# Feed-forward products by one level of Strassen's algorithm, in 1024-token blocks, with activations and weight sums kept in DRAM

## The chip, the cores and the metric

The kernel runs on one core of one Trainium2 chip. The metric is the device time of one execution in microseconds (us), here the median of three runs. The engines are TensorE (PE in the rows, PEld for its weight loads), VectorE (DVE), ScalarE (ACT), GpSimd (POOL) and SyncE (SP, which only issues DMAs). Each engine works through its own instructions in order.

## The reference, cut to what matters

One layer of a decoder trunk with 1024 features, on 2048 tokens with 16 learned tokens ahead of them. Three token mixers and an output projection come first, then the gated feed-forward part, which the change touches. All is float32.

```python
def hybrid_layer(x, ...):
    ...
    x = layer_norm(ALPHA * x + mix, ln1_g, ln1_b)
    u = causal_dwconv(x @ w_up, w_ffn_conv, b_ffn_conv)     # 3 taps, 2 x 2816 channels
    gate, val = jnp.split(u, 2, axis=-1)
    ffn = (jax.nn.silu(gate) * val) @ w_down                # 2816 -> 1024
    return layer_norm(ALPHA * x + ffn, ln2_g, ln2_b)
```

## The kernel before

**Products.** A float32 operand is split into two parts of a rounded type, hi and lo: ScalarE writes hi by a cast (L85), VectorE writes lo by a subtraction (L86); this is `split`. A product of two such operands is three matmuls (`mm3`, L90 to L92): hi by hi, hi by lo, lo by hi, added up in one PSUM bank of 512 columns. Weights come in units of 1024 values per partition (512 KB) by SyncE's queue, three units deep, and are split in halves of 512.

**Mixers.** Four blocks of 512 tokens run through the input projection, the recurrences and the output projection. The output projection and first layer norm of a block come while the next block is at work; that of the last block stands behind all others, in `run_last`. The normalised rows go to a DRAM array `x1`. GpSimd computes in this part alone.

**Feed-forward part.** Per block b of 512 tokens: `load_tokens` reads x1 back and transposes it on TensorE (`transpose_rows`, L172) into eight feature-major tiles `xhi`, `xlo`. `up` makes 22 pairs of a gate tile and a value tile of 128 channels, each 8 contraction tiles by 3 matmuls; in block 0 each is cut in two (258 and 256 columns), since two earlier tokens are needed for the convolution. The convolution's newest tap is ScalarE's (L659), the two others VectorE's (L655), both from the PSUM bank; then swish (L694), a product (L696), and a split into `ahi`, `alo` (for the last eight tiles `chi`, `clo`), all in SBUF. `down` multiplies these with w_down in two halves of 512 output columns, 22 contraction tiles by 4 row tiles by 3 matmuls each, adds to the rows of x1 (L714), and normalises (L194 to L202). In the last block the second half goes in two groups of two row tiles.

**Order.** TensorE's instructions stand in the order in which the program emits them. The other engines' instructions are placed by a scheduler by priority; weights are moved ahead (AHEAD), layer norms behind (BEHIND). `load_tokens(0)` is emitted ahead of `run_last`, so that TensorE works on the last output projection, then at once on `up(0)`.

Of the kernel before, what the change touches and what calls it, by code (L numbers as in the profile page):

```python
# [3 lines left out]

# [19 lines left out]
NB = 4  # L24
# [18 lines left out]


def bcast_rows(row, n):
    """A [1, C] DRAM row read by n partitions."""
    return bass.AP(row.tensor, row.offset, [[0, n], row.ap[-1]])


class Common:  # L50
    """What both phases use: float32r splitting, weight stream, transposes, products, layer norm.

    A float32 operand is split exactly into two float32r parts, hi + lo; a product is
    hi*hi + hi*lo + lo*hi, accumulated in float32.
    """

    def __init__(self, ctx, tc):
# [3 lines left out]
        self.act = ctx.enter_context(tc.tile_pool(name="act", bufs=1))  # L61
        self.wpool = ctx.enter_context(tc.tile_pool(name="w", bufs=3))
        self.rows = ctx.enter_context(tc.tile_pool(name="rows", bufs=5))
# [30 lines left out]
    def load_unit(self, src):  # L94
        """1024 weight values per partition; split in two halves, each in its own step."""
# [62 lines left out]
    def transpose_rows(self, src, t0, n, c0):  # L158
# [4 lines left out]
        nc = self.nc  # L163
        r = min(n, P)
        for k in range(KT):
            if k % 2 == 0:
                xs = self.row_tile().rearrange("p (t c) -> p t c", t=TT)
                nc.scalar.dma_start(
                    xs[0:r, 0:n // r, :], src[t0:t0 + n, k * P:(k + 2) * P].rearrange("(t p) c -> p t c", p=r))
            pt = self.bank()  # L170
            for t in range(n // r):
                nc.tensor.transpose(  # L172
                    pt[:, t * r:(t + 1) * r], xs[0:r, t, (k % 2) * P:(k % 2 + 1) * P], self.ident[0:r, 0:r])
            self.split(self.xT_hi[k][:, c0:c0 + n], self.xT_lo[k][:, c0:c0 + n], pt[:, 0:n])
# [646 lines left out]
```

## Time and profile before

| | us |
|---|---|
| median of three runs (2444.98 to 2448.37) | 2445.55 |
| the profiled execution, first to last instruction | 2445.3 |
| mixers, until the first transpose of `load_tokens(0)` | 885.3 |
| `load_tokens(0)` on TensorE | 15.0 |
| output projection of the last block | 45.4 |
| up, block 0 / each of blocks 1 to 3 | 249.9 / 244.6 |
| down, each of blocks 0 to 2 | 123.2 |
| last down with what follows it | 134.0 |

The page gives the busy time of each engine and the chain of work that ended last. The stages were found from TensorE's timeline, on which each changes its tiles' names, and a table by windows then gives each engine's busy time in each of them. Durations of single instructions come from groups by line and shape. A matmul's own duration includes its pipeline; its pace is the length of a stage over its count.

### The profile page before, as it was taken

To read this page: it belongs to the slowest core of one execution; us is meant where nothing else is said; L and a number is where in the kernel's file an instruction comes from. 1 tells how busy PE (TensorE), PEld (TensorE's weight loads), DVE (VectorE), ACT (ScalarE), POOL (GpSimd) and SP (SyncE) were. 2 spreads that over 40 slices of the span, in tenths; PEclk is the share of its full clock that TensorE was granted. 3 is DMA by queue.
4 is the path that set the end of the run, shared out by engine and by line. 5 is a ranking of instruction groups with operands and counts; after the bars stand their busy time and mean duration, and the time that the engine had idled before them with its cause. 6 is when DMAs were issued, how large, how long until landed. Compare 5 with 4: busy or idle time off the path is not lost.

```text
span 2445.3 us, 33339 instructions
## 1 busy us (share of the span) xinstructions
PE 2410.0 (99%) x12692; PEld 2018.5 (83%) x12692; DVE 1579.6 (65%) x2981; ACT 904.5 (37%) x1646; POOL 318.7 (13%) x351
## 2 busy tenths in 40 slices
PE   8999999999999989999999999999999999999998
PEld 6898777788888879999988888888888888888886
DVE  5676768678867957777635766634766634766636
ACT  3234323422432233554423444422444422444423
POOL 4351424143333310000000000000000000000000
PEclk9999999999999999999999999999999999999999
DMA  5112224322422343422322422322422322422234
GB/s 193 67 60 100 70 70 139 121 78 70 159 93 77 111 132 117 159 96 89 122 94 105 154 95 94 125 93 96 163 94 97 123 95 90 158 96 95 94 109 163
DMA packets 79439, 266.30 MB, mean 109 GB/s; under 512 B 8424, under 2 KB 16896, under 8 KB 79280
## 3 DMA queue, kind: packets, MB, share of 16 engines
q1 hardware_dynamic: 58032, 211.31, 25.0%
q10 hardware_dynamic: 20192, 50.54, 6.0%
q0 software_dynamic: 1056, 2.33, 0.5%
q8 instruction: 99, 1.62, 0.3%
q14 instruction: 60, 0.49, 0.1%
HBM read 247.31 MB, written 16.84 MB: 108 GB/s over the span
## 4 chain that ended last, share of the span: by engine, by line
PE 93%; DVE 3%; POOL 1%; issue 1%; DMA 1%; ACT 0%; DVEq 0%; ACTq 0%; POOLq 0%
PE bank L90 29%; PE bank L91 29%; PE bank L92 29%; PE bank L393 3%; DVE w_lo L86 1%; PE bank L406 1%; PE bank L476 1%; POOL pw L554 1%; PE bank L455 0%; PE bank L477 0%; DVE xlo L86 0%; DVE row L200 0%; DMA row<-x 0%; POOL work L418 0%; POOL work L419 0%
## 5 line engine op out<-in xcount | busy, mean ns | idle before, releaser
L86 DVE TENSOR_TENSOR w_lo<-w_raw,w_hi 128x512 fp32r<-128x512 f32 x806 | 588.2, 730 | 734.1 <-ACT w_hi L85 726.5
L85 ACT CAST w_hi<-w_raw 128x512 fp32r<-128x512 f32 x806 | 499.1, 619 | 1292.4 <-PE bank L92 652.4
L90 PE MATMUL bank<-xhi,w_hi 128*128 128x512 f32 (+3 forms) x2400 | 847.1, 353 | 0.0
L91 PE MATMUL bank<-xlo,w_hi 128*128 128x512 f32 (+3 forms) x2400 | 840.8, 350 | 0.0
L92 PE MATMUL bank<-xhi,w_lo 128*128 128x512 f32 (+3 forms) x2400 | 837.7, 349 | 0.1
L90 PEld LDWEIGHTS bank<-xhi,w_hi 128*128 128x128 f32 x2400 | 452.1, 188 | 64.4 <-issue 0.5
L92 PEld LDWEIGHTS bank<-xhi,w_lo 128*128 128x128 f32 x2400 | 452.0, 188 | 62.3 <-DVE w_lo L86 0.6
L91 PEld LDWEIGHTS bank<-xlo,w_hi 128*128 128x128 f32 x2400 | 451.6, 188 | 60.8 <-issue 0.7
L655 DVE SCALAR_TENSOR_TENSOR y<-bank,f_taps,y 128x256 f32<-128x256 f32 (+4 forms) x528 | 288.4, 567 | 16.3 <-ACT y L659 14.9
L90 PE MATMUL bank<-w_hi,chi 128*128 128x512 f32 (+1 forms) x528 | 211.7, 401 | 0.0
L92 PE MATMUL bank<-w_hi,clo 128*128 128x512 f32 (+1 forms) x528 | 208.0, 394 | 0.0
L91 PE MATMUL bank<-w_lo,chi 128*128 128x512 f32 (+1 forms) x528 | 207.5, 393 | 0.0
L90 PE MATMUL bank<-w_hi,ahi 128*128 128x512 f32 x448 | 177.8, 397 | 0.6 <-DVE xlo L86 0.2
L92 PE MATMUL bank<-w_hi,alo 128*128 128x512 f32 x448 | 177.0, 395 | 0.0
L91 PE MATMUL bank<-w_lo,ahi 128*128 128x512 f32 x448 | 177.0, 395 | 0.0
L659 ACT ACTIVATE y<-bank,f_bias,f_taps 128x512 f32<-128x512 f32 (+1 forms) x220 | 151.2, 690 | 23.9 <-PE bank L92 23.8
L90 PE MATMUL bank<-w_hi,xhi 128*128 128x512 f32 x272 | 112.0, 412 | 7.5 <-ACT xhi L85 7.5
L92 PEld LDWEIGHTS bank<-w_hi,clo 128*128 128x128 f32 (+1 forms) x528 | 97.9, 185 | 24.6
L91 PEld LDWEIGHTS bank<-w_lo,chi 128*128 128x128 f32 (+1 forms) x528 | 98.2, 186 | 22.8
L90 PEld LDWEIGHTS bank<-w_hi,chi 128*128 128x128 f32 (+1 forms) x528 | 98.2, 186 | 21.2
L92 PE MATMUL bank<-w_hi,xlo 128*128 128x512 f32 x272 | 107.7, 396 | 0.0
L91 PE MATMUL bank<-w_lo,xhi 128*128 128x512 f32 x272 | 107.5, 395 | 0.0
(165 smaller groups left out, 2279.5 us busy)
## 6 DMA issues: line engine op xcount, KB each, us to landing
w_raw<-in_w_up_dram SPq DMA_DIRECT2D x176, 512.0 KB, 3.2
w_raw<-in_w_down_dram SPq DMA_DIRECT2D x99, 512.0 KB, 3.2
w_raw<-in_w_feat_dram SPq DMA_DIRECT2D x64, 512.0 KB, 3.3
w_raw<-in_w_rows_dram SPq DMA_DIRECT2D x32, 512.0 KB, 3.3
w_raw<-in_w_o_dram SPq DMA_DIRECT2D x32, 512.0 KB, 3.2
row<-x ACTq DMA_DIRECT2D x32, 512.0 KB, 4.6
row<-in_xT_dram ACTq DMA_DIRECT2D x16, 512.0 KB, 4.6
row<-in_x_dram ACTq DMA_DIRECT2D x16, 512.0 KB, 3.3
```

Source lines behind the costliest of these rows:

```text
L85: self.nc.scalar.copy(hi, src)
L86: self.nc.vector.tensor_sub(lo, src, hi.bitcast(F32))
L90: mm(out, lhsT=a_hi, rhs=b_hi, start=first, stop=False)
L91: mm(out, lhsT=a_hi, rhs=b_lo, start=False, stop=False)
L92: mm(out, lhsT=a_lo, rhs=b_hi, start=False, stop=last)
L393: mm(pt[:, t * P:(t + 1) * P], lhsT=ka[:, c:c + P], rhs=qa[:, c:c + P], start=True, stop=True)
L406: mm(pt[o:o + w, t * P + o + w:t * P + o + 2 * w], lhsT=M[:, c + o:c + o + w], rhs=M[:, c + o + w:c + o + 2 * w], start=True, stop=True)
L476: mm(ot, lhsT=qG[:, c:c + P], rhs=st[:, t, :], start=True, stop=False)
L554: nc.gpsimd.tensor_add(cur[hs, start:W], prev[hs, start:W], prev[hs, start - width:W - width])
L655: self.nc.vector.scalar_tensor_tensor(y, in0=u, scalar=self.taps[:, j, i:i + 1], in1=y, op0=ALU.mult, op1=ALU.add)
L659: self.nc.scalar.activation(y, u, AF.Identity, bias=self.bias[:, j:j + 1], scale=self.taps[:, j, 2:3])
```

## The change

The feed-forward part is written anew (the lines of the new file are meant in what follows; `split` is L102 and L103 there).

Both matrix products are cut into 2 by 2 quarters and made by seven products instead of eight, in Winograd's form: weights and activations are first added up (sums a11, s2, a12, s1, s3, s4, a22 of weights, forms b11, t2, b21, t1, t3, b22, t4 of activations), and the seven products are added up on the way out. Tokens go in two blocks of 1024; a quarter has 512 of them. `up` runs for both blocks, then `down` for both.

- `prepare(0)` reads rows of x1 (256 KB per DMA, issued on ScalarE's queue, two buffers `x_rows`), transposes them (L689, L696), copies them to `x_raw` on ScalarE (L690, L697), makes the four differences on GpSimd (L709 to L712, one buffer `x_t`) and splits seven forms by 4 contraction tiles, in two pieces of 258 and 256 columns. It stands ahead of `run_last`.
- `prepare(1)` does the same for tokens 1024 to 2047 during the first four pairs of `up(0)`, but writes the forms to DRAM (`x_ops1`). `take(1)` loads them between the blocks and makes the 28 splits.
- `weights(j)` loads a gate unit and a value unit, makes four sums of 512 columns on GpSimd (L757 to L760), and splits three operands of 1024 and one of 512.
- `up_pair` makes seven products of 12 matmuls of 512 columns (block 0: 24 of 258 or 256). ScalarE copies the first and third result from the banks (L807, L814), VectorE adds the others (L811 to L828) into SBUF tiles `u`, `cg`, `cv`, of which there is one each. The taps (L838) read SBUF, 1024 wide.
- After every second pair GpSimd makes four sums (L853 to L856, buffer `a_t`), and seven forms of 256 KB go to DRAM (`a_ops`, L860) on SyncE's queue.
- `down_sums` runs beside pairs 4 to 14 of `up(0)`: w_down is loaded in the same four `raw` buffers as w_up, four sums a step are made on GpSimd in `a_t` (L876 to L879) and written to DRAM (`s_ops`, L880).
- `down` loads weights and activations for two contraction tiles at a time (512 KB each, six `raw` buffers) and splits both; the rows of both halves are normalised four at a time.

```diff
+    def prepare(self, b):
+        for k in range(4):
+            ra, rb = self.columns(b, k), self.columns(b, k + 4)
+            for o1, o2, w, at in self.groups(b):
...
+                nc.gpsimd.tensor_sub(t1, ra[:, h2], ra[:, h1])
+                nc.gpsimd.tensor_sub(t2, rb[:, h2], t1)
+                nc.gpsimd.tensor_sub(t3, rb[:, h2], ra[:, h2])
+                nc.gpsimd.tensor_sub(t4, rb[:, h1], t2)
...
+                for i, o in enumerate(X_OPS):
+                    if b == 0:
+                        cm.split(self.x_hi[o][k][:, at:at + w], self.x_lo[o][k][:, at:at + w], ops[o])
+                    else:
+                        nc.sync.dma_start(self.x_dram[b][i, :, k * w:(k + 1) * w], ops[o])
...
+    def product(self, banks, w, o, groups, first):
+        for k in range(4):
+            for i, (wp, xp) in enumerate(((w_hi, self.x_hi), (w_hi, self.x_lo), (w_lo, self.x_hi))):
+                for (_, _, n, at), u in zip(groups, banks):
+                    mm(u[:, 0:n], lhsT=wp[:, kc], rhs=xp[o][k][:, at:at + n], ...)
...
+    def up_pair(self, b, j):
+        self.product(X, w["a11"], "b11", groups, True)       # copied to U
+        self.product(Y, w["s2"], "t2", groups, True)         # U += Y
+        self.product(X, w["a12"], "b21", groups, False)      # copied to cg
+        self.product(A, w["s1"], "t1", groups, True)         # cv = U + A
+        self.product(B, w["s3"], "t3", groups, True)         # cv += B
+        self.product(A, w["s4"], "b22", groups, False)       # cg = U + A
+        self.product(B, w["a22"], "t4", groups, False)       # cv = U + B
...
+    def down_sums(self):
+        for k in range(HK):
+            w1 = self.wpool.tile([P, 1024], F32, tag="raw", name="raw")
+            w2 = self.wpool.tile([P, 1024], F32, tag="raw", name="raw")
...
+            s = self.upool.tile([P, 4, 512], F32, tag="a_t", name="a_t", bufs=1)
...
+            nc.sync.dma_start(self.s_dram[:, :, kc].rearrange("i p c -> p i c"), s)
...
-            drive(load_tokens(cm, x1, 0), pending)
...
-        for b in range(NB):
-            drive(ffn.up(b), pending)
-            if b + 1 < NB:
-                drive(load_tokens(cm, x1, b + 1), pending)
-            drive(ffn.down(b), pending)
...
+                    finish_all([ffn.prepare(0)])
+                    drive(mix.run_last(), pending)
...
+                side = chain(ffn.prepare(1), ffn.down_sums())
+                for b in range(UB):
+                    if b:
+                        finish_all([side])
+                        ffn.take(b)
+                    for _ in ffn.up(b):
+                        next(side, None)
...
+            for b in range(UB):
+                ffn.down(b)
```

**Place 1.** TensorE at the end of the mixers, before: the last transposes of `load_tokens(0)` (`row` holds rows of x1) and the first matmuls of the last output projection (`chi0` and `clo0` are its activations).

```order
L172 MATMUL bank_8135<-ident_78,row_8133 128x128 [waits DMAHW6_49,DVE_49]
L172 MATMUL bank_8135<-ident_78,row_8133 128x128 x3
L172 MATMUL bank_8142<-ident_78,row_8133 128x128 [waits DVE_49]
L172 MATMUL bank_8142<-ident_78,row_8133 128x128 x3
L90 MATMUL bank_8199<-w_hi_8205,chi0_104 128x512 [waits DVE_49]
```

And TensorE there after the change, the last contraction tile of `prepare(0)`.

```order
L689 MATMUL bank_8397<-ident_69,x_pre_8395 128x2 [waits DMAHW0_49,Activation_49]
L696 MATMUL bank_8402<-ident_69,x_rows_8400 128x128 [waits DMAHW1_49,Activation_49]
L696 MATMUL bank_8402<-ident_69,x_rows_8400 128x128 x3
L696 MATMUL bank_8410<-ident_69,x_rows_8408 128x128 [waits DMAHW2_49,Activation_49]
L696 MATMUL bank_8410<-ident_69,x_rows_8408 128x128 x3
L107 MATMUL bank_8462<-w_hi_8468,chi0_88 128x512 [waits Activation_49]
```

Sixteen loads of rows, each with a wait, stand ahead of the output projection where four stood.

**Place 2.** VectorE after the last output projection, before: `row` is being normalised, `w_lo` are up's weights, `y` tiles of `up(0)`.

```order
L86 TENSOR_TENSOR w_lo_8961<-w_raw_8958,w_hi_8960 128x512 [waits DMAHW6_49,PE_49,Activation_49]
L655 SCALAR_TENSOR_TENSOR y_8811<-bank_8812,f_taps_8158,y_8811 128x256 [waits DVE_49]
L202 SCALAR_TENSOR_TENSOR row_8197<-row_8197,ln_rs_8504,ln_b_558 128x1024
L86 TENSOR_TENSOR w_lo_8989<-w_raw_8958,w_hi_8988 128x512 [waits PE_49,Activation_49]
L86 TENSOR_TENSOR w_lo_9032<-w_raw_9029,w_hi_9031 128x512 [waits DMAHW7_49,PE_49,Activation_49]
```

After the change, the end of the same layer norm and the first pair's weights.

```order
L200 SCALAR_TENSOR_TENSOR row_8454<-row_8454,ln_rs_8767,ln_b_561 128x1024 [waits DVE_49]
L200 SCALAR_TENSOR_TENSOR row_8456<-row_8456,ln_rs_8767,ln_b_561 128x1024
L200 SCALAR_TENSOR_TENSOR row_8458<-row_8458,ln_rs_8767,ln_b_561 128x1024 [waits DVE_49]
L198 SCALAR_TENSOR_TENSOR row_8460<-row_8460,ln_mv_8750,ln_g_559 128x1024
L200 SCALAR_TENSOR_TENSOR row_8460<-row_8460,ln_rs_8767,ln_b_561 128x1024 [waits DVE_49]
L103 TENSOR_TENSOR w_lo_8803<-raw_8792,w_hi_8802 128x1024 [waits DMAHW5_49,DMAHW2_49,DMAHW7_49,DVE_49,Activation_49]
```

The layer norm was strewn among the work of `up(0)`; now all of it stands ahead of the first weight split, which waits for the writes of x1 as well.

**Place 3.** VectorE in the middle of `up(0)`, before: `y` are tiles that share weights with nothing else on the way.

```order
L86 TENSOR_TENSOR w_lo_9105<-w_raw_9102,w_hi_9104 128x512 [waits DMAHW1_49,PE_49,Activation_49]
L655 SCALAR_TENSOR_TENSOR y_8882<-bank_8883,f_taps_8158,y_8882 128x2 [waits DVE_49]
L683 COPY f_halo_8162<-bank_8884 128x2
L696 TENSOR_TENSOR y_8882<-y_8811,y_8882 128x512 [waits DVE_49]
L655 SCALAR_TENSOR_TENSOR y_8955<-bank_8956,f_taps_8158,y_8955 128x256 [waits Activation_49]
```

After the change, an odd pair (`u_11189`, `cv_11191`) whose adds stand among the weight splits of the next pair (`raw_11418`, with sums `s_11422`).

```order
L811 TENSOR_TENSOR u_11189<-u_11189,bank_11221 128x256 [waits PE_49,Activation_49]
L103 TENSOR_TENSOR w_lo_11429<-raw_11418,w_hi_11428 128x1024 [waits DMAHW3_49,Activation_49]
L841 TENSOR_TENSOR yv_11142<-yg_11141,yv_11142 128x1024 [waits DVE_49]
L103 TENSOR_TENSOR w_lo_11433<-s_11422,w_hi_11432 128x1024 [waits PE_49,Activation_49]
L818 TENSOR_TENSOR cv_11191<-u_11189,bank_11274 128x256 [waits PE_49]
L818 TENSOR_TENSOR cv_11191<-u_11189,bank_11275 128x256 [waits DVE_49,PE_49]
L103 TENSOR_TENSOR w_lo_11437<-s_11423,w_hi_11436 128x1024 [waits Activation_49]
L822 TENSOR_TENSOR cv_11191<-cv_11191,bank_11302 128x256 [waits DVE_49,PE_49]
```

And GpSimd there: the sums of activations of the two pairs before, a step of `down_sums`, the sums of a pair's weights, and the next step of `down_sums`.

```order
L854 TENSOR_TENSOR a_t_10896<-yv_10887,a_t_10896 128x512 [waits DVE_49,Pool_49]
L855 TENSOR_TENSOR a_t_10896<-yv_10887,yv_10644 128x512
L856 TENSOR_TENSOR a_t_10896<-yv_10887,a_t_10896 128x512 [waits Pool_49]
L876 TENSOR_TENSOR a_t_10914<-raw_10909 128x512 [waits DMAHW3_49,DMAHW4_49,DMAHW1_49,DMAHW5_49,DMAHW0_49,Pool_49]
...
L757 TENSOR_TENSOR s_11167<-raw_11165 128x512 [waits DMAHW5_49,Activation_49]
...
L876 TENSOR_TENSOR a_t_11157<-raw_11152 128x512 [waits DMAHW6_49]
...
L757 TENSOR_TENSOR s_11422<-raw_11420 128x512 [waits DMAHW4_49,DVE_49]
```

GpSimd had nothing in this part before; now it holds a row of sums in which each step reuses the buffer `a_t` of the one ahead, and on whose results VectorE's rows above wait.

## Rows read from the trace of the kernel before

**Rows 1.** The page: busy time by engine, and the chain by engine.

```profile
PE 2410.0 (99%) x12692; PEld 2018.5 (83%) x12692; DVE 1579.6 (65%) x2981; ACT 904.5 (37%) x1646; POOL 318.7 (13%) x351
PE 93%; DVE 3%; POOL 1%; issue 1%; DMA 1%; ACT 0%; DVEq 0%; ACTq 0%; POOLq 0%
```

**Rows 2.** Table by windows: stage, length, busy time (count) by engine, clock, DMA.

```profile
core 0: us, PE busy (x) PEld busy (x) DVE busy (x) ACT busy (x) POOL busy (x), PEclk, DMA share, GB/s
885.30:900.27 14.97, 7.88 (x49) 6.72 (x49) 7.67 (x20) 6.48 (x19) 2.10 (x1) 0.73 0.75 116
900.27:945.67 45.40, 45.40 (x194) 36.95 (x193) 16.45 (x26) 10.02 (x17) 0.00 (x0) 0.97 0.40 139
945.67:1195.59 249.92, 249.92 (x2114) 249.91 (x2112) 189.93 (x455) 125.71 (x222) 1.10 (x2) 1.00 0.34 115
...
1199.43:1322.63 123.20, 123.05 (x528) 99.13 (x529) 39.14 (x60) 28.41 (x47) 0.00 (x0) 1.00 0.31 107
1322.63:1567.27 244.64, 244.64 (x1057) 198.29 (x1056) 177.59 (x366) 111.52 (x178) 0.00 (x0) 1.00 0.32 112
...
2311.34:2445.30 133.96, 122.95 (x529) 98.99 (x527) 66.08 (x100) 42.77 (x69) 0.00 (x0) 0.97 0.38 133
```

**Rows 3.** TensorE's timeline, start, length, idle before: transposes, then the output projection.

```profile
891.44 1.13 PE L172 MATMUL bank<-ident,row 128*128 128x128 f32 x8 [2.12 <-DMA row<-x]
896.98 3.64 PE L172 MATMUL bank<-ident,row 128*128 128x128 f32 x16 [4.40 <-DMA row<-x]
...
901.27 0.63 PE L92 MATMUL bank<-w_hi,clo 128*128 128x512 f32 x1
901.70 0.63 PE L90 MATMUL bank<-w_hi,chi 128*128 128x512 f32 x1
```

**Rows 4.** Groups by shape, VectorE and ScalarE, from 885 us on: busy, mean ns.

```profile
L86 DVE TENSOR_TENSOR w_lo<-w_raw,w_hi 128x512 fp32r<-128x512 f32 x564 | 389.5, 691 | 583.4 <-ACT w_hi L85 579.1 <-PE bank L172 4.1
L194 DVE BATCH_NORM_STATS2 ln_st<-row 128x6 f32<-128x512 f32 x40 | 25.8, 676 | 0.0
L202 DVE SCALAR_TENSOR_TENSOR row<-row,ln_rs,ln_b 128x1024 f32<-128x1024 f32 x20 | 25.4, 1278 | 0.0
L714 DVE SCALAR_TENSOR_TENSOR row<-row,bank 128x512 f32<-128x512 f32 x32 | 20.0, 681 | 2.1 <-PE bank L92 2.1
L85 ACT CAST w_hi<-w_raw 128x512 fp32r<-128x512 f32 x563 | 349.0, 620 | 835.2 <-PE bank L91 431.2 <-PE bank L92 386.9 <-DVE ln_st L194 8.7
```

**Rows 5.** Groups by shape on GpSimd, whole span.

```profile
L418 POOL TENSOR_TENSOR work<-k,work 128x256 f32<-128x256 f32 x84 | 84.1, 1001 | 24.6 <-PE bank L393 12.7 <-PE bank L476 2.9 <-DVE pre L353 2.7
...
L554 POOL TENSOR_TENSOR pw<-pv 128x527 f32<-128x527 f32 x6 | 6.4, 1064 | 0.0
```

**Rows 6.** GpSimd's timeline in the mixers, two instructions.

```profile
328.59 1.29 POOL L382 TENSOR_TENSOR work<-k,work 128x512 f32<-128x512 f32 x1 [10.64 <-ACT work L379]
...
390.14 0.73 POOL L418 TENSOR_TENSOR work<-k,work 128x256 f32<-128x256 f32 x1
```

**Rows 7.** VectorE's timeline at the first of these two.

```profile
328.89 1.54 DVE L86 TENSOR_TENSOR w_lo<-w_raw,w_hi 128x512 fp32r<-128x512 f32 x1
```

**Rows 8.** DMA issues: KB each, median us from issue to landing.

```profile
w_raw<-in_w_up_dram SPq DMA_DIRECT2D x176, 512.0 KB, 3.2
...
row<-x ACTq DMA_DIRECT2D x32, 512.0 KB, 4.6
...
x<-row ACTq DMA_DIRECT2D x16, 512.0 KB, 3.5
```

**Rows 9.** VectorE's and ScalarE's timelines at the end of the span.

```profile
2433.64 1.38 DVE L714 SCALAR_TENSOR_TENSOR row<-row,bank 128x512 f32<-128x512 f32 x2 [2.15 <-PE bank L92]
...
2438.81 2.47 DVE L202 SCALAR_TENSOR_TENSOR row<-row,ln_rs,ln_b 128x1024 f32<-128x1024 f32 x2
...
2440.12 1.53 ACTq L719 DMA_DIRECT2D out_dram<-row  x2
```

More of the change, by code (lines that the diff above doesn't have):

```diff
@@ L3 @@
 from contextlib import ExitStack
+from itertools import chain
 import concourse.bass as bass
@@ L647, in __init__ @@
         self.halo = pool.tile([P, 2 * FT, 2], F32, name="f_halo")
-        own = FT - KT
-        self.hi = [pool.tile([P, TB], F32R, name=f"ahi{j}") for j in range(own)]
-        self.lo = [pool.tile([P, TB], F32R, name=f"alo{j}") for j in range(own)]
-        self.hi += [t[:, 0:TB] for t in cm.cat_hi]
-        self.lo += [t[:, 0:TB] for t in cm.cat_lo]
-    def tap(self, y, u, j, i):
-        self.nc.vector.scalar_tensor_tensor(y, in0=u, scalar=self.taps[:, j, i:i + 1], in1=y,
-                                            op0=ALU.mult, op1=ALU.add)
@@ new lines, in columns @@
+    def columns(self, b, k):
+        nc, cm = self.nc, self.cm
+        raw = self.upool.tile([P, UT + 2], F32, tag="yv", name="x_raw", bufs=2 if b == 0 else 4)
+        fs = slice(k * P, (k + 1) * P)
+        r0 = NM + b * UT
+        if b == 0:
+            xs = self.upool.tile([P, 4, P], F32, tag="x_rows", name="x_pre", bufs=2)[:, 0, :]
+            nc.scalar.dma_start(xs[0:2], self.x1[r0 - 2:r0, fs])
+            pt = cm.bank()
+            nc.tensor.transpose(pt[:, 0:2], xs[0:2], cm.ident[0:2, 0:2])
+            nc.scalar.copy(raw[:, 0:2], pt[:, 0:2])
+        for h in range(UT // 512):
+            xs = self.upool.tile([P, 4, P], F32, tag="x_rows", name="x_rows", bufs=2)
+            nc.scalar.dma_start(xs, self.x1[r0 + h * 512:r0 + (h + 1) * 512, fs].rearrange("(t p) c -> p t c", p=P))
+            pt = cm.bank()
+            for t in range(4):
+                nc.tensor.transpose(pt[:, t * P:(t + 1) * P], xs[:, t, :], cm.ident)
+            nc.scalar.copy(raw[:, 2 + h * 512:2 + (h + 1) * 512], pt)
+        return raw
@@ new lines, in take, with open_up, pool @@
+    def take(self, b):
+        w = UT // 2
+        for i, o in enumerate(X_OPS):
+            for k in range(0, 4, 2):
+                raw = self.wpool.tile([P, 1024], F32, tag="raw", name="raw")
+                self.nc.sync.dma_start(raw, self.x_dram[b][i, :, k * w:(k + 2) * w])
+                for h in range(2):
+                    self.cm.split(self.x_hi[o][k + h][:, 0:w], self.x_lo[o][k + h][:, 0:w], raw[:, h * w:(h + 1) * w])
+    def open_up(self, ctx):
+        def pool(name, bufs):
+            return ctx.enter_context(self.tc.tile_pool(name=name, bufs=bufs, reuse_waits="tile"))
+        self.wpool = pool("f_w", 4)
+        self.upool = pool("f_u", 1)
@@ new lines, in down_product @@
+    def down_product(self, b, p, banks, first):
+        mm = self.nc.tensor.matmul
+        for k0 in range(0, HK, 2):
+            n = min(2, HK - k0)
+            w = self.down_operand(self.source(W_OPS[p], b), k0 * 512, n * 512)
+            a = self.down_operand(self.a_dram[b][p], k0 * 512, n * 512)
+            for k in range(k0, k0 + n):
+                kc = slice((k - k0) * 512, (k - k0 + 1) * 512)
+                w_hi, w_lo = w[0][:, kc], w[1][:, kc]
+                for u, bank in enumerate(banks):
+                    uc = slice((k - k0) * 512 + u * P, (k - k0) * 512 + (u + 1) * P)
+                    a_hi, a_lo = a[0][:, uc], a[1][:, uc]
+                    for i, (x, y) in enumerate(((a_hi, w_hi), (a_hi, w_lo), (a_lo, w_hi))):
+                        mm(bank, lhsT=x, rhs=y, start=first and k == 0 and i == 0, stop=k == HK - 1 and i == 2,
+                           skip_group_check=True)
@@ L722, in load_tokens @@
-def load_tokens(cm, x1, b):
-    if b == 0:
-        yield from cm.transpose_rows(x1, NM - 2, 2, NM - 2)
-    yield from cm.transpose_rows(x1, NM + b * TB, TB, NM)
+        nu = 4
+        add = nc.vector.tensor_add
+        rows = []
+        for t in range(2 * nu):
+            r = self.dpool.tile([P, D], F32, tag="row", name="row", bufs=2 * nu + 2)
+            t0 = b * UT + t * P
+            nc.sync.dma_start(r, self.x1[NM + t0:NM + t0 + P, :])
+            nc.scalar.mul(r, r, ALPHA)
+            rows.append(r)
@@ new lines, in down, with banks, onto @@
+        f1, f2 = slice(0, 512), slice(512, 1024)
+        us = [self.dpool.tile([P, 512], F32, tag="du", name="du", bufs=nu + 2) for _ in range(nu)]
+        def banks():
+            return [cm.bank() for _ in range(nu)]
+        def onto(part, f, bs):
+            for u in range(nu):
+                add(rows[part * nu + u][:, f], rows[part * nu + u][:, f], bs[u])
+        A = banks()
+        self.down_product(b, 0, A, True)
+        for u in range(nu):
+            nc.scalar.copy(us[u], A[u])
@@ new lines, in down @@
+        B = banks()
+        self.down_product(b, 1, B, True)
+        for u in range(nu):
+            add(us[u], us[u], B[u])
+            for t, f in ((u, f2), (nu + u, f1), (nu + u, f2)):
+                nc.gpsimd.tensor_add(rows[t][:, f], rows[t][:, f], us[u])
+        self.down_product(b, 2, A, False)
+        onto(0, f1, A)
+        C = banks()
+        self.down_product(b, 3, C, True)
+        onto(1, f2, C)
+        E = banks()
+        self.down_product(b, 4, E, True)
+        onto(1, f2, E)
@@ L729, in drive, with finish @@
+        self.down_product(b, 5, C, False)
+        onto(1, f1, C)
+        self.finish(b, rows[nu:], nu)
+        self.down_product(b, 6, E, False)
+        onto(0, f2, E)
+        self.finish(b, rows[:nu], 0)
+    def finish(self, b, rows, t0):
+        self.cm.layer_norm(rows, P)
+        for t, r in enumerate(rows):
+            o = b * UT + (t0 + t) * P
+            self.nc.scalar.dma_start(self.out[o:o + P, :], r)
 def drive(main, pending):
```

283 lines of the change are left out of this document (191 added, 92 removed).

## The prediction

> **What bounds the kernel now.** I read the page first: TensorE is busy 99% of the span and holds 93% of the chain [rows 1]; nothing else is near. Then the table by stage [rows 2]: in up and down TensorE's busy time equals the length of the stage, so each stage is its count of matmuls times a pace. Up of block 0 has 2112 matmuls in 249.9 us, 0.1183 each (258 or 256 columns); of another block 1056 in 244.6, 0.2317 each; a down 528 in 123.2, 0.2333 each. The one stage where TensorE idles is the reload of tokens at 885 us (7.9 of 15.0 us busy), where it waits for rows from DRAM [rows 2, 3]. Fewer matmul columns therefore pay in full, if TensorE stays fed; what has to be costed is what feeds it.
>
> **TensorE's own gain.** Up now has 44 pairs of 7 products. Block 0: 22 x 7 x 24 = 3696 narrow matmuls x 0.1183 = 437.3. Block 1: 22 x 7 x 12 = 1848 x 0.2317 = 428.2. Together 865.5 against 249.9 + 3 x 244.6 = 983.7: -118.2. Down: 1848 x 0.2333 = 431.2 against 2112 x 0.2333 = 492.8: -61.6. Sum -179.8. A pair takes 19.9 us (block 0) or 19.5 (block 1), a product 2.8. The shapes and operands are those of before, so I keep the paces. Transposes are as many as before.
>
> **Ahead of the output projection, +50.** The changed order puts all of `prepare(0)` on TensorE before the last output projection, which began at 900.3. The chain of one contraction tile is serial: load rows, transpose, copy, load the other half's rows (ScalarE issues these only behind its copies), transpose, copy, then seven GpSimd differences until the buffers come free, with splits between. A load lands in 3.2 to 4.6 us [rows 8]; the nearer row is that of reading x1, but of twice the size, so I take 3.9. A transpose of 128 columns is 0.14 [rows 3], four 0.5; a copy 0.6 [rows 4]; a difference of 256 columns 0.73 when alone and 1.0 on the mean [rows 5, 6]. 2 x 3.9 + 2 x 0.5 + 2 x 0.6 + 7 x 0.73 + some 1.6 of splits = 16.7. From about 890, three such turns and the first 10 us of the fourth end at 950: +50, from +44 (loads at 3.2) to +61 (loads at 4.6 or differences at 1.0).
>
> **Behind it, +22.** `up(0)` used to cover the last layer norm. Now the first weight split stands behind it on VectorE and waits for the rows' writes. Four adds at 0.68, six statistics at 0.67, eight passes of 1024 columns at 1.28 [rows 4] are 17, the write 3.5 [rows 8], a 1024-wide cast (two of 0.62) 1.2, and the second product waits somewhat for its sums: 22, from 20 to 26. GpSimd's sums of the first weights wait for the same writes, which is where the second product's wait comes from.
>
> **In up of block 0, +40.** Let p be a GpSimd operation of 512 columns: 1.06 (an add of 527) to 1.29 [rows 5, 6]. In pairs 6 to 15 the activations' sums and `down_sums` share one buffer, `down_sums` and w_up share four raw buffers, and VectorE's adds of an odd pair stand behind the splits of the next pair's weights. That closes a loop over two pairs: from the odd pair's result, 3p of sums; their write, 2.8 (bounded by 3.5 for twice the size [rows 8]); 4p of `down_sums`, which frees the raw buffers; a load of two units, 3.2 and about 0.9; 4p of weight sums; 4p of the next `down_sums`; a load, 4.1; 3p of the next pair's sums; cast and split, 2.5; adds, 0.9; the two last products, 5.7; adds, taps and product behind them (five passes of 1.28 or less), 6.6. In all 26.6 + 18p = 45.7 to 49.8, where TensorE needs 39.7. Five turns: +30 to +51, I take +40. In the other pairs weights are a pair or more ahead and I charge nothing. Their cover is VectorE's and GpSimd's time: a pair costs VectorE three splits and six passes at 1.28 or less, one split at 0.69 and five adds at 0.68, some 14.3 us, and GpSimd six operations, 6.4 to 7.7, both under 19.5.
>
> The trace shows that the two do not run freely side by side: a split that takes 0.69 alone [rows 4] took 1.54 when it began 0.3 us into a GpSimd product of 1.29 [rows 6, 7]; it waited out most of it. The Trainium skill ("SBUF — State Buffer", "Who interferes with whom") says why: a VectorE instruction with two SBUF inputs contends with a GpSimd instruction that reads SBUF, under an exclusive lock. The trace agrees, and by that rule alone the 10.9 us of VectorE's two-SBUF-input work would share one port with GpSimd's 6.4 to 7.7, 17.3 to 18.6 a pair, still under TensorE's pace; the sum stays. What more than that would do is the second rival.
>
> **Between the blocks, +17.** `take(1)` gives VectorE 28 splits in its queue ahead of the next pair's first. The last forms can only be overwritten behind the last products, so some ten splits of 0.69, the last pair's taps (five passes) and one weight split come after the last product, 15; the weights' raw buffers come free late, so their load (3.2) and sums add a little. 13 to 20, I take 17.
>
> **Up to down, +7; the end, +7.** Down's first splits stand behind the last pair's taps: an add, three taps, two splits of 1.28, 7 (5 to 10). At the end four rows are normalised behind the last product instead of two. Before, 11.7 us lay between the last product and the end [rows 9]; two rows more add two adds, four statistics and four passes, 9, less what drains while the last banks finish: +7 (6 to 9). Between these ends down takes 1 MB and two 1024-wide splits per two contraction tiles, 5.6 us of TensorE: 2.6 of VectorE, and 190 GB/s, against 139 in a stage at DMA share 0.40 [rows 2]; no charge.
>
> **Restarts, +3.** After the idle at 885 the granted clock is 0.73 in that window [rows 2] and the first matmuls come 0.43 apart instead of 0.23 [rows 3], about 1 us a time; three long idles are new.
>
> **The sum.** The profiled execution is 2445.3, the median 2445.55, so no correction: 2445.3 - 179.8 + 50 + 22 + 40 + 17 + 7 + 7 + 3 = 2411.5. All low ends give 2383, all high ends 2446.
>
> **Rivals.** *The covers hold.* If the loads of `prepare(0)` overlap (+25 instead of 50) and the loop does not close, since the scheduler's order leaves slack I don't see (0 instead of 40), the time is 2411 - 65 = 2346. For it: DMA is busy 0.3 to 0.4 in every stage [rows 2]. Against it: the waits are written into the order, and single buffers can't overlap. *Shared port, slower.* If each GpSimd operation holds up VectorE for its whole length, adds from PSUM behind a held split too, a pair costs 14.3 + 6.4 to 7.7 = 20.7 to 22.0. It decides from 19.5 on. Block 1 then loses 1.2 to 2.5 a pair, 27 to 56; the twelve free pairs of block 0 0.8 to 2.1, 10 to 26; the loop pairs (28.6 and 20 operations, 50 to 54 per two) 10 to 32 more: 2459 to 2525, middle 2490. For it: rows 6 and 7. Against it: GpSimd needs only a third of a pair, and some of its work falls beside VectorE's adds from PSUM. *Long round trips, slower.* If the new DRAM traffic lands in twice the time (eight loads in `prepare(0)`, three steps a loop turn), +28 and +50: 2490. The rows show no such time; against it speaks the DMA share.
>
> **Chances.** Forecast, 2383 to 2440: 0.46. Covers hold: 0.18, which with the forecast is faster. Within 0.2% of before (5 us, about what a measurement of this kernel can tell from no change): 0.08, the forecast's upper end. Slower: 0.28, shared port 0.17, round trips 0.11. The range leaves out the lower part of the first rival and the upper parts of the others: 2335 to 2490.
>
> **What would show it.** Right: TensorE idle about 60 us between 885 and 950, 22 before the first L780 matmul of up, some 8 per two pairs in pairs 6 to 15 with VectorE's L818 behind L103 splits, none in block 1, 17 between the blocks; paces of 0.118, 0.232, 0.233. Wrong: idle spread over block 1's pairs with L103 splits near 2 us (shared port); output projection by 930, no idle in block 0 (covers); down's matmuls spaced above 0.24 (its feed is short, which I charged at nothing).

## The result, and the profile after

The changed kernel takes 2517.2 us (median of 4 runs, 2511.8 to 2517.5) against 2445.3 for the kernel before on the same chip: slower by 2.8% (ratio 1.028, 95% interval 1.027 to 1.030). The profiled execution is 2510.0 us long, 98.5 above the forecast of 2411.5.

First the page of the changed kernel, busy time by engine.

```profile
PE 2299.7 (92%) x12692; PEld 1962.0 (78%) x12692; DVE 1680.1 (67%) x2284; ACT 892.5 (36%) x1407; POOL 899.0 (36%) x819
```

Against [rows 1], TensorE has 110 us less to do, and the span is 65 longer: its idle time went from 35 us to 210. GpSimd works 899 us instead of 319. Where the idle time lies is told by the table by windows of the changed kernel (columns as in [rows 2]): `prepare(0)`, output projection, the wait before up, then of block 0 the pairs 0 to 3 and 6 to 15, of block 1 the stretch from its first pair's second half to its last pair, that last pair with the change to down, then down, and the end.

```profile
core 0: us, PE busy (x) PEld busy (x) DVE busy (x) ACT busy (x) POOL busy (x), PEclk, DMA share, GB/s
885.00:944.82 59.82, 19.62 (x83) 14.01 (x81) 25.35 (x52) 27.48 (x73) 18.36 (x25) 0.54 0.25 73
944.82:990.20 45.38, 45.38 (x193) 36.93 (x192) 20.33 (x33) 12.56 (x26) 5.91 (x7) 0.97 0.21 70
990.20:1013.41 23.21, 0.55 (x3) 0.13 (x1) 15.38 (x22) 1.39 (x3) 4.98 (x4) 0.62 0.45 149
1013.41:1131.10 117.69, 98.82 (x737) 96.80 (x737) 66.16 (x80) 45.58 (x64) 49.28 (x41) 0.89 0.43 145
...
1181.71:1468.82 287.11, 236.79 (x1682) 229.01 (x1681) 165.57 (x191) 83.77 (x112) 163.75 (x122) 0.89 0.44 142
...
1627.00:2024.00 397.00, 397.00 (x1716) 321.85 (x1715) 299.30 (x285) 165.32 (x182) 186.13 (x160) 1.00 0.29 98
2024.00:2049.41 25.41, 19.91 (x87) 15.79 (x86) 15.81 (x17) 9.32 (x11) 2.75 (x5) 0.95 0.50 186
2049.41:2491.80 442.39, 429.88 (x1847) 349.66 (x1848) 271.68 (x281) 175.69 (x194) 53.16 (x27) 0.98 0.63 212
2491.80:2510.00 18.20, 0.39 (x2) 0.00 (x0) 14.52 (x21) 0.30 (x1) 0.00 (x0) 0.56 0.28 116
```

Block 1 is as reckoned: TensorE is busy in all of the 397 us shown, 0.2314 a matmul. The loss is in block 0: 594.3 us from its first product to that of block 1, where 437.3 of products stand. Pair by pair it took

```
pair  0    1    2    3    4    5    6    7    8    9    10   11   12   13   14   15
us   31.1 30.7 28.1 27.8 20.4 30.2 21.9 38.5 21.1 37.1 20.5 37.2 20.4 37.6 20.6 32.3
pair  16   17   18   19   20   21   22   23   24   25 to 42     43
us   21.3 20.3 20.3 20.3 20.3 36.3 27.6 19.5 19.5 19.4 or 19.5  25.1
```

(start of a pair's first product to start of the next one's, from TensorE's timeline). So there are the odd pairs 7 to 15, the first four pairs, pair 5, and the change of blocks at 21 and 22. TensorE's timeline of the changed kernel, with the waits (start, length, instruction, idle before and releaser), shows the first product of up and the start of its second, 5.7 us later, then one of each sort:

```profile
1013.41 0.80 PE L780 MATMUL bank<-xb11h,w_hi 128*128 128x258 f32 x2 [22.66 <-ACT w_hi L102]
...
1019.13 0.61 PE L780 MATMUL bank<-xt2h,w_hi 128*128 128x258 f32 x2
...
1042.88 1.94 PE L696 MATMUL bank<-ident,x_rows 128*128 128x128 f32 x8 [5.11 <-DMA x_rows<-x]
...
1164.54 0.86 PE L780 MATMUL bank<-xb21h,w_hi 128*128 128x258 f32 x2 [7.09 <-ACT u L807]
...
1234.67 0.91 PE L780 MATMUL bank<-xb22h,w_hi 128*128 128x258 f32 x2 [4.29 <-DVE cv L818]
...
1607.72 0.79 PE L780 MATMUL bank<-xb11h,w_hi 128*128 128x512 f32 x1 [15.80 <-ACT w_hi L102]
```

The row at 1234.67 is the wait that the prediction named: the sixth product of an odd pair waits for VectorE's adds, which stand behind the next pair's weight splits. GpSimd's timeline shows what the splits were waiting for there (the first row: weight sums that begin 6.5 us late, behind a load), and then the turn that follows.

```profile
1226.30 2.12 POOL L757 TENSOR_TENSOR s<-raw 128x512 f32<-128x512 f32 x1 [6.52 <-DMA raw<-in_w_up_dram]
...
1251.85 1.28 POOL L856 TENSOR_TENSOR a_t<-yv,a_t 128x512 f32<-128x512 f32 x1
1255.64 1.28 POOL L876 TENSOR_TENSOR a_t<-raw 128x512 f32<-128x512 f32 x1 [2.50 <-DMA a_ops<-a_t]
...
1259.50 1.29 POOL L879 TENSOR_TENSOR a_t<-raw,a_t 128x512 f32<-128x512 f32 x1
...
1264.96 1.81 POOL L757 TENSOR_TENSOR s<-raw 128x512 f32<-128x512 f32 x1 [3.92 <-DMA raw<-in_w_up_dram]
...
1270.51 2.28 POOL L876 TENSOR_TENSOR a_t<-raw 128x512 f32<-128x512 f32 x1
1272.74 2.26 POOL L878 TENSOR_TENSOR a_t<-raw 128x512 f32<-128x512 f32 x1
1274.96 1.71 POOL L877 TENSOR_TENSOR a_t<-a_t,raw 128x512 f32<-128x512 f32 x1
1276.75 2.13 POOL L879 TENSOR_TENSOR a_t<-raw,a_t 128x512 f32<-128x512 f32 x1
```

It is the predicted chain step by step: sums of activations, 2.5 us until their write frees `a_t`, `down_sums`, 3.9 us for the load that had waited for its buffers, weight sums, the next `down_sums`. What is different is the length of an operation: 1.28 where VectorE is idle or adds from a PSUM bank, up to 2.28 where it is at work on SBUF operands alone. Two rows of VectorE's timeline, one of each kind:

```profile
1256.71 0.75 DVE L822 TENSOR_TENSOR cv<-cv,bank 128x256 f32<-128x256 f32 x2 [2.09 <-PE bank L780]
...
1270.32 3.54 DVE L103 TENSOR_TENSOR w_lo<-s,w_hi 128x1024 fp32r<-128x1024 f32 x2 [4.37 <-ACT w_hi L102]
```

### The profile page after: what moved, and what is told of

Read it like the earlier page. It is cut to its first block, busy times and chain, and to the rows that moved or that the text cites. A ratio compares the mean times of both kernels' runs of the same rounds, so it can differ in the third digit from the quotient of the medians.

```text
span 2510.0 us, 33594 instructions
## 1 busy us (share of the span) xinstructions
PE 2299.7 (92%) x12692; PEld 1962.0 (78%) x12692; DVE 1680.1 (67%) x2284; ACT 892.5 (36%) x1407; POOL 899.0 (36%) x819
## 5 line engine op out<-in xcount | busy, mean ns | idle before, releaser
L103 DVE TENSOR_TENSOR w_lo<-raw,w_hi 128x1024 fp32r<-128x1024 f32 x212 | 265.8, 1290 | 173.6 <-ACT w_hi L102 172.6
L102 ACT CAST w_hi<-raw 128x1024 fp32r<-128x1024 f32 x212 | 202.1, 993 | 459.1 <-PE bank L915 221.7
L102 ACT CAST w_hi<-w_raw 128x512 fp32r<-128x512 f32 x256 | 158.3, 619 | 481.9 <-PE bank L109 281.5
L103 DVE TENSOR_TENSOR w_lo<-w_raw,w_hi 128x512 fp32r<-128x512 f32 x256 | 208.6, 816 | 171.6 <-ACT w_hi L102 165.8
L915 PE MATMUL bank<-w_hi,w_lo 128*128 128x512 f32 x616 | 243.6, 395 | 9.1 <-DVE w_lo L103 8.9
L915 PE MATMUL bank<-w_hi 128*128 128x512 f32 x616 | 242.4, 394 | 8.8 <-ACT w_hi L102 8.8
L915 PE MATMUL bank<-w_lo,w_hi 128*128 128x512 f32 x616 | 242.1, 393 | 0.1
L107 PE MATMUL bank<-xhi,w_hi 128*128 128x512 f32 (+1 forms) x640 | 234.4, 366 | 0.0
L103 DVE TENSOR_TENSOR w_lo<-s,w_hi 128x1024 fp32r<-128x1024 f32 x88 | 141.5, 1609 | 108.9 <-ACT w_hi L102 108.5
L102 ACT CAST w_hi<-s 128x1024 fp32r<-128x1024 f32 x88 | 92.3, 1050 | 222.7 <-PE bank L780 130.5
L109 PEld LDWEIGHTS bank<-xhi,w_lo 128*128 128x128 f32 x640 | 120.3, 188 | 17.4 <-DVE w_lo L103 0.5
L107 PEld LDWEIGHTS bank<-xhi,w_hi 128*128 128x128 f32 x640 | 120.4, 188 | 16.4 <-issue 0.7
L108 PEld LDWEIGHTS bank<-xlo,w_hi 128*128 128x128 f32 x640 | 120.8, 189 | 15.0 <-issue 0.7
L757 POOL TENSOR_TENSOR s<-raw 128x512 f32<-128x512 f32 x44 | 75.4, 1714 | 152.0 <-DMA raw<-in_w_up_dram 51.6
L838 DVE SCALAR_TENSOR_TENSOR yg<-cg,f_taps,yg 128x1024 f32<-128x1024 f32 x88 | 118.0, 1341 | 13.1 <-ACT yg L835 12.5
L838 DVE SCALAR_TENSOR_TENSOR yv<-cv,f_taps,yv 128x1024 f32<-128x1024 f32 x88 | 118.6, 1348 | 6.9 <-issue 3.3
```

The source lines that it names most:

```text
L102: self.nc.scalar.copy(hi, src)
L103: self.nc.vector.tensor_sub(lo, src, hi.bitcast(F32))
L107: mm(out, lhsT=a_hi, rhs=b_hi, start=first, stop=False)
L108: mm(out, lhsT=a_hi, rhs=b_lo, start=False, stop=False)
L109: mm(out, lhsT=a_lo, rhs=b_hi, start=False, stop=last)
L757: nc.gpsimd.tensor_add(sa[:, h:], wv[:, 0:h], wv[:, h:])
```

## The experiments

Each experiment but the last two is a single execution. Its span is compared with the 2510.0 us of the changed kernel's profile; four executions of the changed kernel lay up to 5.7 us apart, so a difference in span of that size shows nothing by itself.

**Does the stall travel with the sums of w_down?** The eleven steps are moved from block 0 to block 1.

```diff
-                side = chain(ffn.prepare(1), ffn.down_sums())
+                side = ffn.prepare(1)
...
                         ffn.take(b)
+                        side = ffn.down_sums()
```

> The same work, with the eleven steps of down_sums beside the first eleven pairs of block 1 instead of pairs 4 to 14 of block 0. Theory (closed loop): the stall belongs to the loop of single and shared buffers (a_t, raw) and the sums on GpSimd, so it travels: block 0's odd pairs 7 to 15 fall from 37 us to about 20.5, and two-pair turns of 50 us or more (39 without the loop) appear in the first eleven pairs of block 1; the span stays within 25 us of 2510. Rival (block 0's form: narrow matmuls, more instructions per pair, VectorE and GpSimd both fuller): the odd pairs of block 0 stay above 30 us or the stall does not appear in block 1 at all; the span falls by 60 us or more.

The span is 2516.3. Pairs 5 to 20 of block 0 all take 20.3; odd pairs of block 1 from 25 to 33 take 34 to 36. The table by windows of this run, ten pairs of block 0 and eleven of block 1:

```profile
1179.03:1382.30 203.27, 203.27 (x1683) 203.27 (x1681) 153.97 (x191) 82.85 (x111) 83.84 (x80) 1.00 0.28 98
1520.14:1823.00 302.86, 247.27 (x924) 190.38 (x924) 166.70 (x150) 88.15 (x97) 170.38 (x127) 0.88 0.43 141
```

The first shows TensorE without a pause; the same ten pairs took 287 in the changed kernel, with the same products. The stall belongs to the loop, not to block 0's narrow matmuls; the rival falls. Pair 5's 10 us went too: that stall was the loop's first turn.

**Do GpSimd's operations lie on the loop's path?** Each sum in a step of `down_sums` is made twice.

```diff
             nc.gpsimd.tensor_add(s[:, 0, :], a21, a22)
+            nc.gpsimd.tensor_add(s[:, 0, :], a21, a22)
```

(and so for the three others)

> Each of the four sums in a step of down_sums is made twice on GpSimd, with the same result. A turn of two pairs holds two such steps. Theory (GpSimd's operations lie end to end on the loop's path): eight more operations of 1.3 to 1.8 us lengthen a turn from 58 to between 68 and 72, so the odd pairs from 37 to 48 or more, and the span by 50 to 75. Rival (the turn's long part is loads and VectorE's order, GpSimd has slack inside it): turns stay below 62, the span grows by less than 25.

Turns of two pairs take 68.3 us (57.4 in the changed kernel), the span 2579.1. The table by windows, five turns:

```profile
1194.23:1535.67 341.44, 242.51 (x1682) 234.01 (x1681) 176.25 (x192) 84.22 (x112) 229.00 (x164) 0.82 0.36 120
```

That is the theory's turn (68 to 72) and span (69 more); the odd pairs, at 45, lie below its 48. Eight added operations cost 10.9 us a turn, 1.4 each. TensorE's busy time is within 6 us of the changed kernel's; GpSimd's is 65 longer over the five turns, and the stretch 54, so most of it is on the path. The rival, slack inside the turn, falls.

**The same sums on VectorE.** First all of them, then those of w_up alone.

```diff
-            nc.gpsimd.tensor_add(sa[:, h:], wv[:, 0:h], wv[:, h:])
+            nc.vector.tensor_add(sa[:, h:], wv[:, 0:h], wv[:, h:])
```

(all twelve sums in `weights`, `up` and `down_sums`; in the second run only the four in `weights`)

> All sums of weights, of activations and of down_sums on VectorE instead of GpSimd, in the same places; only the differences of the x forms stay on GpSimd. Theory (the loop's time is 26.6 us plus 18 GpSimd operations, which take 1.3 to 2.3 us each since they and VectorE hold each other up): at 0.69 each the loop is 39 us, about TensorE's 39.7; the turns of two pairs fall from 58 us to 40 to 45, and the span by 60 to 90. Rival (VectorE has no room, or the loads are the loop's long part): VectorE becomes the bound at 21 us a pair with nothing gained in the odd pairs, turns stay above 52 us, the span falls by less than 30 or grows.

> Only the sums of w_up on VectorE; those of activations and of down_sums stay on GpSimd. A turn of the loop holds seven of them among its 18 operations. Theory (each operation in the chain counts with its own length): seven times 1.6 less 0.7 is 6 us, so the turns of two pairs fall from 58 to about 52, between the changed kernel and the run with all sums on VectorE (46); span 2470 to 2490. Rival (what counts is that the two engines hold each other up at all, and any GpSimd work left keeps the turn): turns stay at 56 or more, span above 2500.

With all of them on VectorE a turn takes 46.6 us and the span is 2454.0; the theory is just missed: 56 less instead of 60 to 90, and a turn above its 40 to 45. By the table by windows over the five turns, VectorE is now busy 199 of 233 us, 19.9 a pair:

```profile
1180.99:1414.01 233.02, 213.49 (x1682) 209.01 (x1681) 198.70 (x294) 83.93 (x112) 9.79 (x20) 0.98 0.53 174
```

So the rival may have a part in it: what is left of the stall goes with a VectorE that is nearly full, though no run shows that this is its cause. With w_up's sums alone a turn is 55.0 and the span 2509.0: the theory's 52 was wrong, and of the rival's two numbers the span holds and the turn (56) just does not. Block 1 took back most of what the turns gained: ten of its pairs now take 20.4 us instead of 19.4. GpSimd's groups by shape in that run, and what their first line waited for, show where the gain went in block 0:

```profile
L876 POOL TENSOR_TENSOR a_t<-raw 128x512 f32<-128x512 f32 x9 | 14.1, 1571 | 40.4 <-DMA s_ops<-a_t 20.3 <-DMA a_ops<-a_t 11.2 <-issue 6.5
```

```profile
  DMA s_ops<-a_t: 20.3, 3
```

Its first sum of `down_sums` now waits three times, 6.8 us each, for the write of the step before to free `a_t`; in the changed kernel no such wait stands in the turns, since GpSimd was at the weight sums meanwhile. Seven operations were taken out of the path, and a wait of nearly 7 us came in; the loop has more than one path of nearly the same length.

**One step of the sums per two pairs.** All on GpSimd, through both blocks.

```diff
             nc.sync.dma_start(self.s_dram[:, :, kc].rearrange("i p c -> p i c"), s)
             yield
+            yield
...
-                        finish_all([side])
                         ffn.take(b)
...
+                finish_all([side])
```

> One step of down_sums per two pairs instead of one per pair, through both blocks; all on GpSimd as in the changed kernel. Theory (closed loop): a turn loses four operations and one load, 58 less 6 to 8 less 4 to 6, so 44 to 48 us a turn, over eleven turns instead of five and a half; the price per step of down_sums falls from about 8 us to 5 and the span by 20 to 45. Rival (any step of down_sums costs an odd pair its 17 us): eleven stalls of 17 us, span above 2560.

Turns are 44.4 us in block 0, the span 2461.9, 48 less: the theory, a little beyond its range. A step costs an odd pair about 4 us now, pair 5 among them (24.8 instead of 30.2). This is the smallest of the changes to the loop, and leaves the work where it was.

**The reload of block 0's tokens.** Its steps go between those of the output projection, a step after each.

```diff
-                    finish_all([ffn.prepare(0)])
-                    drive(mix.run_last(), pending)
+                    prep = ffn.prepare(0)
+                    for _ in mix.run_last():
+                        next(prep, None)
+                    finish_all([prep])
```

(with a yield after each half of `columns`)

> The steps of prepare(0) stand between the steps of the last output projection on TensorE, one pair of tiles of transposes after each, instead of all ahead of it. Theory (the reload is a chain of loads, copies and differences that TensorE need not wait for): output projection and prepare(0) together take 60 to 70 us from 885 instead of 105, up begins near 978 instead of 1013, and the span falls by 30 to 40. Rival (the chain's end or the layer norm's wait moves with it): up begins no earlier than 1000.

The output projection ends at 956.5 instead of 990.2, 34 earlier, but up begins at 988.1, only 25 earlier. TensorE's timeline of this run at that place:

```profile
988.12 0.80 PE L786 MATMUL bank<-xb11h,w_hi 128*128 128x258 f32 x2 [30.92 <-ACT w_hi L102]
```

Eight of the 34 come back as a longer wait, 31 instead of 23 us: what follows the output projection no longer stands alone on VectorE, where ten splits of token forms now stand between the adds and the layer norm, the first of them here:

```profile
957.49 0.41 DVE L103 TENSOR_TENSOR xt2l<-x_t,xt2h 128x258 fp32r<-128x258 f32 x1
```

The span is 2493.9, so 16 less, about half of what the theory had; its 978 for the start of up is missed by 10, and the rival's 1000 isn't reached. Block 0 lost another 6, which was not traced.

**The transposes of block 1's tokens in smaller steps.** Eight steps of two tiles instead of four of four.

```diff
-            ra, rb = self.columns(b, k), self.columns(b, k + 4)
+            ra = self.columns(b, k)
+            if b:
+                yield
+            rb = self.columns(b, k + 4)
```

> prepare(1) in eight steps of two transposed tiles instead of four steps of four, so that the rows for the next step can be loaded during a pair; down_sums moves four pairs later. Theory (TensorE waits in the first four pairs because the second half of a step's rows is loaded only when the first half's transposes are done): transposes and waits between pairs fall from 7 us a step to 2 in each of eight, pairs of 22 to 24 instead of 28 to 31, and the span falls by 10 to 25. Rival (the rows land late anyway): eight gaps of 5 us or more, span 2510 or above.

Pairs 0 to 7 take 21.2 to 24.2 us; the first four lost 28 us in sum, the next four got 6 longer by transposes of their own. TensorE's timeline at the first of them has no wait any more:

```profile
1037.01 1.04 PE L696 MATMUL bank<-ident,x_rows 128*128 128x128 f32 x8
1037.80 0.49 PE L783 MATMUL bank<-xb11h,w_hi 128*128 128x258 f32 x2
```

The span is 2493.4, 17 less, as the theory had it. The loop, moved four pairs on, is as long as before (pairs 9, 11, 13, 15: 37 to 39), and its first turn, which cost pair 5 only 10 us, is now a full one.

**Are narrow products slow because they alternate banks?** The undisturbed pairs of block 0 took 20.3 us, where 19.9 were reckoned.

```diff
-        for k in range(4):
...
-                for (_, _, n, at), u in zip(groups, banks):
+        for (_, _, n, at), u in zip(groups, banks):
+            for k in range(4):
```

> In block 0 the two column pieces of a product run one after the other (12 matmuls each), as in the kernel before, instead of alternating from matmul to matmul. Theory (alternating the banks costs the narrow matmuls 0.003 us each, 0.121 against 0.118): undisturbed pairs of block 0 fall from 20.3 to 19.9 us and the span by up to 10. Rival (the pace is set by something else, the weight loads or the 258th column): no change, 20.3 us a pair.

Pairs take 20.2, the span is 2504.4: the theory falls. Why the narrow matmuls come 0.121 us apart and not 0.118 stays open; it is worth 10 us.

**Together.** All sums on VectorE, the reload between the steps of the output projection, the transposes in eight steps, one step of `down_sums` per two pairs.

> Together: all sums on VectorE, prepare(0) between the steps of the output projection, prepare(1) in eight steps, one step of down_sums per two pairs. Theory: the terms found so far add up. Up begins 25 earlier; turns of two pairs at 40.6, that is no stall in block 0 beyond the first pairs (from 594 us to about 480); block 1 with one step in two pairs 19.5 to 21 a pair; in all 2510 less 25, 80 to 100 and 10, 2370 to 2400, faster than the kernel before by 2 to 3%. Rival (VectorE, with some 20 us of work a pair, becomes the bound in both blocks): pairs of 21 to 23 throughout, 2420 to 2460, about as before.

It takes 2389.1 us (median of 4) against 2447.2 for the kernel before, ratio 0.977 (0.975 to 0.979): faster than both, and within the theory's range, though turns in block 0 are 43.6 us, not 40.6. The table by windows: until up, up of block 0, of block 1, down.

```profile
885.00:982.67 97.67, 60.48 (x278) 47.03 (x276) 58.42 (x106) 42.18 (x102) 24.85 (x32) 0.82 0.37 115
982.67:1476.78 494.11, 465.05 (x3760) 458.90 (x3760) 427.58 (x607) 207.37 (x287) 52.27 (x62) 0.98 0.45 155
1476.78:1921.91 445.13, 433.63 (x1848) 348.37 (x1848) 386.63 (x453) 180.88 (x200) 15.61 (x44) 0.99 0.35 120
1921.91:2365.68 443.77, 429.50 (x1848) 349.15 (x1848) 272.70 (x284) 175.81 (x194) 47.61 (x24) 0.99 0.63 212
```

Block 0 is 100 us shorter than in the changed kernel, and VectorE, at 428 of 494 and 387 of 445 us, looked like the next bound. So I gave the sums of w_up back to GpSimd, with all else kept.

> As the run that put the changes together, but the sums of w_up back on GpSimd, those of activations and of down_sums on VectorE. Theory (with one step of down_sums per two pairs the loop has slack, and it is VectorE's 20 us a pair that stretched pairs to 20.7 to 22 there): pairs of block 0 from the ninth on at 20.3, of block 1 at 19.5, span 2355 to 2375. Rival (GpSimd and VectorE hold each other up again as soon as both read SBUF): pairs as long as before or longer, span 2385 to 2420.

That is the rival, and more than its 2385 to 2420: 2447.3 us (median of 10), ratio to the kernel before 1.000 (0.999 to 1.001). The groups by shape on VectorE and GpSimd, 1200 to 1400 us, first of the run before, then of this one:

```profile
L846 DVE SCALAR_TENSOR_TENSOR yv<-cv,f_taps,yv 128x1024 f32<-128x1024 f32 x18 | 23.1, 1283 | 1.1
L849 DVE TENSOR_TENSOR yv<-yg,yv 128x1024 f32<-128x1024 f32 x9 | 11.0, 1219 | 0.0
```

```profile
L846 DVE SCALAR_TENSOR_TENSOR yv<-cv,f_taps,yv 128x1024 f32<-128x1024 f32 x18 | 31.7, 1760 | 0.9
L849 DVE TENSOR_TENSOR yv<-yg,yv 128x1024 f32<-128x1024 f32 x9 | 16.6, 1846 | 0.8
...
L767 POOL TENSOR_TENSOR s<-raw 128x512 f32<-128x512 f32 x9 | 18.9, 2095 | 0.0
```

The same instructions, with the same shapes, take 1.76 and 1.85 us instead of 1.28 and 1.22 as soon as GpSimd's sums run beside them, and a GpSimd sum takes up to 2.1 on the mean. The table by windows of this run, up of block 0 and of block 1:

```profile
991.00:1523.70 532.70, 480.04 (x3760) 473.70 (x3761) 428.28 (x519) 206.62 (x287) 195.12 (x146) 0.94 0.42 143
1523.70:1986.97 463.27, 440.10 (x1849) 352.31 (x1849) 369.96 (x365) 180.09 (x200) 155.50 (x132) 0.97 0.34 116
```

VectorE has 176 instructions fewer than in the run before, some 120 us at 0.68 each, but its busy time fell by only 16 us, from 814 to 798: the rest of its work became longer by nearly all that was taken off it. The list of waits has a second cause, first as it was in the run before, then in this one:

```profile
DVE a_t L884 <- DMA a_ops<-a_t: 6.1, 8, 1.6
```

```profile
DVE a_t L884 <- DMA a_ops<-a_t: 36.5, 9, 4.8
```

VectorE's sums of `down_sums` wait nine times, 4 us on the mean, for the write that frees `a_t`, and VectorE's other work stands behind them. In the run before, VectorE had the sums of w_up to make meanwhile. How the 60 us divide between the two was not separated.

No run gave the loop a second buffer `a_t` or more `raw` buffers, so what the buffers alone are worth is not shown.

## Why the prediction was wrong, point by point

It was wrong in direction and outside its range. The places were named rightly, but for the first four pairs; the steps that failed are sizes and two charges of nothing. The differences below add up to about the 98.5 us.

- **TensorE's own gain** was right: block 1 0.2314 a matmul, a down product 30.8 us for 132 matmuls, 0.2333. Only the narrow matmuls were slower, 0.121 (+10 us).
- **Ahead of the output projection** +50 was forecast, it began at 944.8, +44.5. **Behind it** 22, measured 23.2. Both right.
- **The loop in block 0** is the main failed step. Its course was right, as the three runs show that moved, doubled and thinned out the sums, but a turn took 57.4 us instead of 47.8, and five turns cost 84 us over undisturbed pairs instead of 40. The sum took an operation of 512 columns from 1.06 to 1.29. The upper end is the length without VectorE beside it (1.26 to 1.29 in the turn shown); the lower was an add of another shape, and no sum of the loop was ever so short. In that turn (58.1 us) the eighteen on the path took 27.5 us, 1.53 each, where the sum's middle had 21.2: over 6 of its 10 us. Of the rest, 2.5 are the second load of a turn, 6.6 us instead of 4.1: two loads of 512 KB are issued 0.4 us apart, with the 1 MB write of the sums right behind them. (That wait is 6.4 to 6.6 in the four full turns; in two of them the profile puts it down to a VectorE split that ended as late. Why the load took so long was not tested.) Another 1.6 are the first of the two products after the wait, which runs at the lower of the clock's two levels. The rows that told of it were in front of me: [rows 6, 7], which I applied to the sum of work per pair and not to the length of each step of a chain, and two rows of the view of [rows 5] that were left out:

```profile
L429 POOL TENSOR_TENSOR work<-k,work 128x512 f32<-128x512 f32 x12 | 17.7, 1473 | 7.4 <-PE bank L393 6.5
L382 POOL TENSOR_TENSOR work<-k,work 128x512 f32<-128x512 f32 x12 | 16.8, 1398 | 204.5 <-ACT work L379 140.4 <-DVE k L357 51.1 <-issue 12.3
```

They give operations of 512 columns at 1.40 and 1.47 on the mean in the mixers. With 1.45 the prediction's own sum comes to 52.7 a turn (an estimate from these rows).

- **"In the other pairs I charge nothing"** is the second failed step. `prepare(1)`'s transposes stand in TensorE's order, and its rows were loaded a half step too late: 28.8 us in four gaps where 11.5 of transposes, all three reloads together, were in the kernel before. The first products of pairs 0 to 3 took another 8 at the lower clock, 2.8 of them behind the wait before up. It is the same trap as `prepare(0)`, which I had priced.
- **Restarts +3** was too small: the first products of pairs 0 to 3 alone cost 8, and a turn of the loop 1.6 (both counted above). Over the five turns TensorE's busy time was 33 us longer than for the same products without a pause (236.8 against 203.3), but most of that is hidden in a turn whose length the chain sets.
- **Pair 5**, 10 us: the first turn of the loop, which I had put at pair 6.
- **Between the blocks** 17 was forecast; pairs 21 and 22 took 24 more than undisturbed ones, above its 13 to 20. Up to down 5.6 (forecast 7), the end 18.2 after the last product (18.7): right.
- **Down "no charge"**: +11 us over its products. Thirteen of the 14 products have a wait of 0.3 to 3.3 us at their start for their first splits.
- **The rivals.** The shared port was given 2459 to 2525, and the result lies there, but not by the mechanism told: block 1, where it should have cost 27 to 56 us, kept TensorE's pace with GpSimd's sums at 1.3 to 2.3 us. The Trainium skill ("SBUF — State Buffer", "Who interferes with whom") has it that a VectorE instruction with two SBUF inputs contends with a GpSimd instruction that reads SBUF. The traces here agree: a GpSimd sum goes from 1.28 to 2.28 us beside VectorE, and VectorE's tap from 1.28 to 1.76 beside GpSimd. What that costs hung here on whether a chain ran through both engines: it did in the turns of block 0, and not in block 1. "The covers hold" was wrong, and so were the long round trips as they were told: the loads in the turns were waited for 3.9 to 6.6 us, not twice as long in general.
- **Slips that change no term:** VectorE's cover counts six passes a pair; there are five, and its 14.3 comes out with five. The +61 of `prepare(0)` needs slow loads and slow differences together, not one of them.

## What to carry to other kernels

A share of busy time says whether an engine can carry its work; it says nothing of a chain in which buffers are passed round. Where single buffers close a loop over several engines, write the loop out step by step, and price each step with its length under the load that will be beside it. Take that length from rows where the other engine is at work, not from the shortest row there is. Extra work that is needed only later (here a step of `down_sums`) costs less when it is spread: 57.4 us a turn with two steps, 44.4 with one. And work that moves to another engine takes its waits along, or uncovers those that it had hidden.

## What the runs showed of the hardware

VectorE's and GpSimd's work on SBUF lengthens both: in the rows above a GpSimd sum goes from 1.28 to as much as 2.28 us, and VectorE's passes of 1024 columns from 1.28 and 1.22 to 1.76 and 1.85 on the mean. VectorE's adds from PSUM kept their length (0.41 us on the mean for 256 columns in every run).

The narrow matmuls' pace of 0.121 us, with weight loads busy all the time, was 0.118 in the kernel before with the same shapes; exchanging the loop order did not bring it back.

In stretches where TensorE idled, the granted clock lay between its two levels, 1.2 and 2.4 GHz: 0.89 of the upper over the turns, 0.62 in the wait before up. The first product of up, after 22.7 us of idle, took 5.7 us instead of 2.9, its matmuls 0.21 us apart instead of 0.12. So a stage that is cut up by waits pays more than its idle time, where TensorE is on the path.
